# Moving the affine map of five norms from GpSimd to VectorE, one stage later, in a two-block transformer kernel

## The chip, the cores and the metric

The kernel runs on one core of a Trainium2 chip, in one launch. The metric is the device time of one execution in microseconds (us); lower is better. Times are medians of several executions. Five engines share the work: TensorE (PE in the rows; the loading of its stationary operand is PEld), VectorE (DVE), ScalarE (ACT), GpSimd (POOL) and SyncE (SP), which here only issues DMAs. Each engine executes its own instructions in order and waits on semaphores for the others.

## What is computed

512 tokens of 1024 channels go through six residual stages with a layer norm each (a first block of depth 2) and then through a second block whose details the change does not touch:

```python
for i in range(2):
    y = mla(x) if i == 0 else dsa(x)            # latent attention / sparse attention
    x = layer_norm(ALPHA * x + y, ln_g[i, 0], ln_b[i, 0])
    y = memory_cross_attention(x, mem, ...)     # 4 heads of 256 over 256 memory tokens
    x = layer_norm(ALPHA * x + y, ln_g[i, 1], ln_b[i, 1])
    y = swiglu_ffn(x, ...)
    x = layer_norm(ALPHA * x + y, ln_g[i, 2], ln_b[i, 2])
return second_block(x, ...)                     # modulation, gated attention and pooling, conv FFN, final norm
# layer_norm(x, g, b) = (x - mean) * rsqrt(var + eps) * g + b
```

All of it is float32. Every large product is made of three passes with operands split into a high and a low part (`wh`/`wl` for weights), so that the product keeps float32 precision.

## The kernel before

The residual stream `xs` is four tiles of [128 tokens, 1024]. The output projection of a stage (`out_proj`, called by `block_out` or, for the last one of the first block, by `run`) has the tokens on the partitions. It runs over all k but the last five (eight for that last one) with the four token tiles side by side in PSUM, and then finishes the tiles one by one, so that a tile's statistics, norm and transposes lie beside the products of the next tile. `ln_stats` adds the residual to the product (`x<-x,acc`, line 203) and takes mean and variance on VectorE; `ln_rest` has ScalarE normalise the tile in place. The tile is then (x - mean) * rstd, without g and b.

The gain and the shift are then applied twice, to two copies. The transposed copy `xT`, which feeds the next stage's products, gets them by feature when it is evicted (`t_group`, ScalarE). The residual tiles themselves get them by `affine`, lines 748 to 751: for each tile one multiply by `lg` (line 750) and one add of `lb` (line 751), both [128, 1024] float32 on GpSimd. `lg` and `lb` are rows broadcast over the partitions, and `ln_rows` (lines 744, 745) loads them by DMA from ScalarE's queue. Nothing reads the affine residual tiles before the next output projection adds them to its product, except the sparse attention, which stores them to DRAM (`spill`, line 1072, SP's queue), frees their pages, and reloads them with `xload` (line 737) at its end.

`affine` is called in five places for the first block's norms 0 to 4: twice in `xa` (the cross attention), twice in `ffn`, and once in `dsa`. In the program's order it stands behind the last step of `xa`, and behind `fm_first` (the first four products of a stage) in `ffn` and `dsa`. The Tile scheduler places it by its dependencies; on GpSimd nothing else stands ahead of it in `xa`.

Weights arrive in 512 KB pages on SP's queue (`raw`), ScalarE rounds them to `wh` (line 121) and VectorE subtracts to get `wl` (line 122; in some stages GpSimd does it). `use` and `ensure` keep four units prepared ahead of TensorE. `split` does the same to activations: ScalarE casts (lines 160 or 163), VectorE subtracts (lines 161 or 164). In `xa` the steps are: four head-halves of q by `fm_first`, then `s1(h)` (scores, line 155 among others, row maximum on VectorE, exponential on ScalarE), `norm(h)` (line 876, VectorE), `s2(h)` (transposes, split) and `s3(h)` (values).

Of the kernel before, what the change touches and what calls it, by code (L numbers as in the profile page):

```python
# [14 lines left out]
OP = mybir.AluOpType  # L15
# [16 lines left out]
# where steps of the memory's keys and values go between the heads (MLA) or the blocks of queries (sparse attention),  # L32
# and where the products of the second half's values (MLA) and of the pooled channels go between the heads
# [31 lines left out]
class K:  # L65
# [29 lines left out]
    def after(self, inst, prev):  # L95
        """Keep inst behind prev on their engine."""
        self.tc.add_manual_dep(inst.ins, prev.ins.name,
                               mybir.DependencyInfo(mybir.DependencyClass.NoSync, mybir.DependencyReason.SCHED_ONLY),
                               reason="order")

# [66 lines left out]
    def rsqrt_ops(self, v, n, eps, ops, out):  # L167
        """out = (v + eps) ** -0.5 on [128, n], as a list of steps."""
# [42 lines left out]
    def ln_rest(self, mv, x):  # L211
        """Steps from the statistics to the normalised tile."""
# [8 lines left out]
    def t_group(self, xs, xT, grp, gb):  # L221
        """Steps: transposes of token tiles 2*grp, 2*grp+1, then the affine map by feature, then the split."""
# [35 lines left out]
    def out_proj(self, nk, lhs, stats, rest, xT, tr, gb, last=5):  # L258
        """lhs(k): function of the token tile, the two parts; tr: the tiles that are transposed."""
# [6 lines left out]
        for k in range(nk - last):  # L266
            lp = lhs(k)
            u = self.use()
            for t in range(NT):
                mm(t, k, lp, u)  # L270
        lps = [lhs(k) for k in range(nk - last, nk)]
        us = [self.use(0) for _ in range(last)]
        self.ensure(self.cur + 4)

# [24 lines left out]
    def fm_first(self, xT, xs, gb, jobs):  # L299
        """jobs: functions(ps) that take the finished [128, 512] product."""  # L300
# [46 lines left out]
    def trig(self):  # L347
        """cos and signed sin of the rotary angles, [128 = (.., 2, 16), S]."""
# [25 lines left out]
    def rope(self, src, out):  # L374
        """Rotate [128 = (4, 2, 16), S] (in PSUM or SBUF), split into the pair out."""
# [284 lines left out]
    def attention(self, nh, rows, vals, OT, scale, ahead, before3=None, fill=None, lag=3):  # L660
        """Causal attention of heads of 64."""
# [86 lines left out]
    def affine(self, xs, rows):  # L748
        for x in xs:
            self.nc.gpsimd.tensor_tensor(x, x, rows[0], op=OP.mult)  # L750
            self.nc.gpsimd.tensor_tensor(x, x, rows[1], op=OP.add)
# [13 lines left out]
    def block_out(self, n, nk, lhs, xs):  # L765
        """Output product, residual and norm n; the normalised tiles stay in xs, their transposes begin."""
# [3 lines left out]
                      xT, xs, gb)  # L770
        return xT, gb

# [58 lines left out]
    def fill(self, n=1):  # L831
        """Some steps of the memory's keys and values, between other work."""
# [10 lines left out]
    def xa(self, i, xT, xs, gb, KT, V):  # L843
# [9 lines left out]
        rows = self.ln_rows(3 * i)  # L853
# [67 lines left out]
        self.affine(xs, rows)  # L921
        return OT

# [1 line left out]
    def ffn(self, xT, xs, gb, rows=None, step=None, conv=None):  # L925
# [32 lines left out]
        if rows is not None:  # L958
            self.affine(xs, self.ln_rows(rows))
# [95 lines left out]
    def dsa(self, xT, xs, gb):  # L1055
# [13 lines left out]
        self.affine(xs, self.ln_rows(2))  # L1069
# [25 lines left out]
        # scores of the keys, and their choice  # L1095
# [55 lines left out]
        # keys, values, queries  # L1151
# [34 lines left out]
        # attention: rows (4 groups of 4 queries, 4 queries, 2 key heads, 4 query heads of each), 16 queries at a time  # L1186
# [5 lines left out]
        def qblk(s):  # L1192
            """The queries of 64 tokens by blocks, as steps."""
# [132 lines left out]
    def bias_tables(self):  # L1326
        """Thresholds by (query % 4, bucket) and group of 4 queries; steps of the bias table in three bfloat16 parts,
        one block for each query."""
# [49 lines left out]
    def second(self, xT, xn, xs):  # L1378
# [9 lines left out]
        # pooling over trailing windows  # L1388
# [23 lines left out]
        # forget gates  # L1412
# [23 lines left out]
        # values  # L1436
# [117 lines left out]
    def run(self):  # L1554
# [12 lines left out]
        xT, gb = self.block_out(1, 8, self.cols(OT), xs)  # L1567
# [4 lines left out]
        lhs = self.ffn(xT, xs, gb, 1, self.mod_step)  # L1572
        xT, gb = self.block_out(2, NF, lhs, xs)
# [4 lines left out]
        xT, gb = self.block_out(3, 8, lhs, xs)  # L1578
# [4 lines left out]
        xT, gb = self.block_out(4, 8, self.cols(OT), xs)  # L1583
# [4 lines left out]
        lhs = self.ffn(xT, xs, gb, 4, self.mod_step)  # L1588
# [15 lines left out]
        self.out_proj(NF, lhs, lambda t, acc: self.ln_stats(t, acc, xs[t]), rest, xT, xn, self.modgb(0), 8)  # L1604
# [9 lines left out]
def layout(inputs):  # L1614
    """The arrays that the program reads: inputs, some with their rows or columns regrouped, and constants."""
# [45 lines left out]
```

## Time and profile before

| | before |
|---|---|
| runs | 2223.41, 2224.93, 2235.49 us; median 2224.93 us |
| span of the profiled execution | 2221.3 us |
| median over that span | 3.6 us |
| TensorE busy | 2153.8 us (97%) |
| VectorE busy | 1378.0 us (62%) |
| ScalarE busy | 899.0 us (40%) |
| GpSimd busy | 415.9 us (19%) |

The profile's own execution has no time beside its span; the 3.6 us are what the median of the runs has above it, start and end of the execution included. All positions below are microseconds from the span's start. The stages that the change touches lie at 320 to 375 us (first cross attention) and 375 to 415 (its output projection), 415 to 700 and 700 to 785 (first feed-forward and its output projection), 815 to 1110 and 1114 to 1160 (sparse attention), 1186 to 1240 and 1240 to 1285 (second cross attention), 1285 to 1534 and 1534 to 1650 (second feed-forward). A row of a group names the engine, the line, the operation, the tile written and the tiles read. In the timeline a bracket gives how long the engine had been idle before the instruction and what it had waited for. PEclk is the granted clock of TensorE as a share of 2.4 GHz.

### The profile page before, as it was taken

Reading aid. Unit: us, or ns where it says so; the run is one execution under the profiler, and the core shown is the slowest. Engines: PE = TensorE matmul, PEld = TensorE weight load, DVE = VectorE, ACT = ScalarE, POOL = GpSimd, SP = SyncE. Lnnn points to the kernel's source line nnn. Section 1 sums busy time; section 2 is a strip of 40 time slices with the busy share of each in tenths; the row PEclk is TensorE's granted clock in tenths of the full one; section 3 lists DMA queues with packets and bytes.
Section 4 is the critical chain, followed back from the end, with each engine's and each line's share of the span. In section 5 each row is a group of like instructions: output and inputs, shape, how many; then the busy total and the mean of one; then the engine's idle time right before and its main releaser. Section 6 shows DMA issues by size and latency. Waiting matters only on the chain.

```text
span 2221.3 us, 30434 instructions
## 1 busy us (share of the span) xinstructions
PE 2153.8 (97%) x11668; PEld 1806.4 (81%) x11668; DVE 1378.0 (62%) x2779; ACT 899.0 (40%) x1636; POOL 415.9 (19%) x330
## 2 busy tenths in 40 slices
PE   8899998999999999889998999999999999999998
PEld 7789897888888887776588898888888879888886
DVE  5776567575335269898866575435477676755633
ACT  3687344322234143456633342224323555433521
POOL 0355112040000024365504030000004210000002
PEclk9999999999999998999999999999999999999999
DMA  5223622264324214231242336544410144433311
GB/s 194 57 65 101 196 81 90 71 203 145 103 86 142 63 45 123 64 113 39 81 133 76 95 113 209 162 134 142 114 49 22 52 124 143 125 104 95 123 67 39
DMA packets 253394, 232.29 MB, mean 105 GB/s; under 512 B 14656, under 2 KB 219840, under 8 KB 253248
## 3 DMA queue, kind: packets, MB, share of 16 engines
q1 hardware_dynamic: 246240, 213.93, 31.4%
q10 hardware_dynamic: 7008, 16.41, 2.3%
q8 instruction: 92, 1.51, 0.3%
q14 instruction: 54, 0.44, 0.1%
HBM read 220.80 MB, written 6.82 MB: 102 GB/s over the span
## 4 chain that ended last, share of the span: by engine, by line
PE 82%; DVE 8%; issue 2%; ACT 1%; POOL 1%; DMA 0%; ACTq 0%; DVEq 0%; POOLq 0%
PE fm L154 13%; PE fm L153 13%; PE fm L155 13%; PE acc L154 9%; PE acc L153 9%; PE acc L155 9%; DVE wl L122 1%; PE v L153 1%; PE o L153 1%; PE v L154 1%; PE o L154 1%; PE v L155 1%; PE o L155 1%; PE s L1232 1%; PE s L155 1%
## 5 line engine op out<-in xcount | busy, mean ns | idle before, releaser
L154 PE MATMUL fm<-xT,wh 128*128 128x512 f32 (+3 forms) x1640 | 590.6, 362 | 0.4
L155 PE MATMUL fm<-xT,wl 128*128 128x512 f32 (+3 forms) x1640 | 589.9, 360 | 0.0
L153 PE MATMUL fm<-xT,wh 128*128 128x512 f32 (+3 forms) x1640 | 589.6, 361 | 0.1
L122 DVE TENSOR_TENSOR wl<-raw,wh 128x1024 fp32r<-128x1024 f32 (+1 forms) x299 | 399.7, 1365 | 113.2 <-ACT wh L121 75.0
L121 ACT CAST wh<-raw 128x1024 fp32r<-128x1024 f32 (+2 forms) x339 | 338.7, 1039 | 62.9 <-PE acc L154 19.7
L154 PEld LDWEIGHTS fm<-xT,wh 128*128 128x128 f32 (+2 forms) x1640 | 308.4, 188 | 48.4 <-DVE xT L250 1.6
L155 PEld LDWEIGHTS fm<-xT,wl 128*128 128x128 f32 (+2 forms) x1640 | 308.7, 188 | 47.3
L153 PEld LDWEIGHTS fm<-xT,wh 128*128 128x128 f32 (+2 forms) x1640 | 307.8, 188 | 48.0 <-DVE xT L249 0.4
L153 PE MATMUL acc<-wh,hs 128*128 128x512 f32 x528 | 205.6, 389 | 0.0
L155 PE MATMUL acc<-wh,hs 128*128 128x512 f32 x528 | 205.4, 389 | 0.0
L154 PE MATMUL acc<-wl,hs 128*128 128x512 f32 x528 | 205.4, 389 | 0.0
L750 POOL TENSOR_TENSOR x<-x,lg 128x1024 f32<-128x1024 f32 x20 | 60.5, 3045 | 720.8 <-DMA lg<-in_ln_g_dram 625.9
L122 POOL TENSOR_TENSOR wl<-raw,wh 128x1024 fp32r<-128x1024 f32 (+1 forms) x40 | 94.0, 2359 | 409.9 <-DVE ss L1370 327.5
L955 DVE TENSOR_TENSOR hT<-sil,fm 128x512 f32<-128x512 f32 x44 | 30.2, 686 | 194.7 <-PE fm L155 194.7
L954 ACT ACTIVATE sil<-fm 128x512 f32<-128x512 f32 x44 | 26.3, 599 | 293.9 <-PE fm L155 285.3
L938 DVE SCALAR_TENSOR_TENSOR cv<-fm,cw,cv 128x511 f32<-128x511 f32 x88 | 65.7, 748 | 81.9 <-ACT cv L936 80.7
L155 PEld LDWEIGHTS acc<-wh,hs 128*128 128x128 f32 x528 | 99.1, 188 | 20.6
L153 PEld LDWEIGHTS acc<-wh,hs 128*128 128x128 f32 x528 | 99.1, 188 | 20.6
L154 PEld LDWEIGHTS acc<-wl,hs 128*128 128x128 f32 x528 | 99.1, 188 | 20.4
L153 PE MATMUL acc<-wh,ot 128*128 128x512 f32 x288 | 112.5, 391 | 0.0
L155 PE MATMUL acc<-wh,ot 128*128 128x512 f32 x288 | 112.1, 389 | 0.0
L154 PE MATMUL acc<-wl,ot 128*128 128x512 f32 x288 | 112.0, 389 | 0.0
(366 smaller groups left out, 3738.0 us busy)
## 6 DMA issues: line engine op xcount, KB each, us to landing
raw<-in_ffn_w_in_dram SPq DMA_DIRECT2D x88, 512.0 KB, 4.0
mw<-in_mod_w_dram SPq DMA_DIRECT2D x48, 512.0 KB, 4.5
raw<-in_ffn_w_down_dram SPq DMA_DIRECT2D x44, 512.0 KB, 3.3
raw<-in_ffn_up_dram SPq DMA_DIRECT2D x44, 512.0 KB, 4.0
raw<-in_xa_w_kv_dram SPq DMA_DIRECT2D x32, 512.0 KB, 3.9
raw<-in_ffn_down_dram SPq DMA_DIRECT2D x22, 512.0 KB, 3.3
raw<-in_xa_w_q_dram SPq DMA_DIRECT2D x16, 512.0 KB, 5.8
raw<-in_xa_w_o_dram SPq DMA_DIRECT2D x16, 512.0 KB, 3.8
```

Of the source, the lines that this page charges most:

```text
L121: self.nc.scalar.copy(hi[:, :n], raw[:, :n])
L122: self.lo_eng.tensor_tensor(lo[:, :n], raw[:, :n], hi[:, :n].bitcast(F), op=OP.subtract)
L153: mm(out, l[0], r[0], start=first, stop=False, **kw)
L154: mm(out, l[0], r[1], start=False, stop=False, **kw)
L155: mm(out, l[1], r[0], start=False, stop=last, **kw)
L750: self.nc.gpsimd.tensor_tensor(x, x, rows[0], op=OP.mult)
L938: nc.vector.scalar_tensor_tensor(y[:, sh:], p[:, :S - sh], w[:, 2 - sh, c:c + 1], y[:, sh:], op0=OP.mult, op1=OP.add)
L954: nc.scalar.activation(s, g, AF.Silu)
L955: nc.vector.tensor_tensor(hT[j // 2][:, j % 2], s, u, op=OP.mult)
L1232: mm(p[32 * gq:32 * gq + 32, 0:nk], D3[:, i, hf], mv[:, gq, 0:nk], start=False, stop=i == 2, skip_group_check=True)
```

## The change

`affine` moves to VectorE. `xa`, `ffn` and `dsa` no longer call it; instead `out_proj` takes a list `pre` with one step for each tile. It executes one step after each k of its first loop and the remaining ones ahead of the products that finish the tiles. The rows `lg` and `lb` are loaded where the output projection begins. In `dsa` the tiles are now spilled without the affine map, and get it after the reload. The core of the diff (comments and docstrings, which the change also removes, left out, so lines behind them move by a few):

```diff
     def affine(self, xs, rows):
         for x in xs:
-            self.nc.gpsimd.tensor_tensor(x, x, rows[0], op=OP.mult)
-            self.nc.gpsimd.tensor_tensor(x, x, rows[1], op=OP.add)
+            self.nc.vector.tensor_tensor(x, x, rows[0], op=OP.mult)
+            self.nc.vector.tensor_tensor(x, x, rows[1], op=OP.add)
+
+    def affine_of(self, xs, n):
+        if n is None:
+            return None
+        rows = self.ln_rows(n)
+        return lambda t: self.affine(xs[t:t + 1], rows)
...
-    def out_proj(self, nk, lhs, stats, rest, xT, tr, gb, last=5):
+    def out_proj(self, nk, lhs, stats, rest, xT, tr, gb, last=5, pre=None):
+        pre = [] if pre is None else [lambda t=t, f=pre: f(t) for t in range(NT)]
...
             for t in range(NT):
                 mm(t, k, lp, u)
+            if pre:
+                pre.pop(0)()
         lps = [lhs(k) for k in range(nk - last, nk)]
         us = [self.use(0) for _ in range(last)]
         self.ensure(self.cur + 4)
+        for f in pre:
+            f()
...
-    def block_out(self, n, nk, lhs, xs):
+    def block_out(self, n, nk, lhs, xs, prev=None):
...
-                      xT, xs, gb)
+                      xT, xs, gb, pre=self.affine_of(xs, prev))
...
         self.fm_first(xT, xs, gb, [take(m) for m in range(4)])      # xa
-        rows = self.ln_rows(3 * i)
...
         s3(3)
-        self.affine(xs, rows)
...
-        if rows is not None:                                        # ffn
-            self.affine(xs, self.ln_rows(rows))
...
         self.fm_first(xT, xs, gb, [take_qi(m) for m in range(4)])   # dsa
-        self.affine(xs, self.ln_rows(2))
         spill = self.tc.dram_tile([NT, 128, D], F, name="spill")
...
-        xT, gb = self.block_out(1, 8, self.cols(OT), xs)
+        xT, gb = self.block_out(1, 8, self.cols(OT), xs, 0)
...
-        lhs = self.ffn(xT, xs, gb, 4, self.mod_step)
+        lhs = self.ffn(xT, xs, gb, self.mod_step)
+        pre = self.affine_of(xs, 4)
         rows = self.ln_rows(5)
```

What this does to the order of the instructions: TensorE's order stays as it was but for one exchange of neighbours. GpSimd loses the 40 instructions of lines 750 and 751; VectorE gains 40 of the same shape (lines 756 and 757 in the changed file).

The first place is VectorE in the output projection of the first cross attention. `ot` are the last splits of the attention, `wl` the low parts of weights: the first four (from raw_3628 to raw_3964) are units 4 to 7 of this projection, the other four belong to the next stage. Before:

```order
543 L161 TENSOR_TENSOR ot_3931<-o_3924,ot_3931 128x512
544 L161 TENSOR_TENSOR ot_3941<-o_3934,ot_3941 128x512
545 L122 TENSOR_TENSOR wl_3961<-raw_3628,wh_3960 128x1024
546 L122 TENSOR_TENSOR wl_3991<-raw_3714,wh_3990 128x1024
547 L122 TENSOR_TENSOR wl_4021<-raw_3766,wh_4020 128x1024
548 L122 TENSOR_TENSOR wl_4051<-raw_3964,wh_4050 128x1024
549 L122 TENSOR_TENSOR wl_4057<-raw_3994,wh_4056 128x1024
550 L122 TENSOR_TENSOR wl_4063<-raw_4024,wh_4062 128x1024
551 L122 TENSOR_TENSOR wl_4069<-raw_4054,wh_4068 128x1024
552 L122 TENSOR_TENSOR wl_4075<-raw_4060,wh_4074 128x1024
553 L203 SCALAR_TENSOR_TENSOR x_2836<-x_2836,acc_3952 128x512
```

And now, where the same four units are wl_3953, wl_3985, wl_4017 and wl_4049:

```order
544 L161 TENSOR_TENSOR ot_3937<-o_3930,ot_3937 128x512
545 L756 TENSOR_TENSOR x_2836<-x_2836,lg_3940 128x1024
546 L122 TENSOR_TENSOR wl_3953<-raw_3624,wh_3952 128x1024
547 L757 TENSOR_TENSOR x_2836<-x_2836,lb_3941 128x1024
548 L122 TENSOR_TENSOR wl_3985<-raw_3710,wh_3984 128x1024
549 L756 TENSOR_TENSOR x_2838<-x_2838,lg_3940 128x1024
550 L122 TENSOR_TENSOR wl_4017<-raw_3762,wh_4016 128x1024
551 L757 TENSOR_TENSOR x_2838<-x_2838,lb_3941 128x1024
552 L756 TENSOR_TENSOR x_2840<-x_2840,lg_3940 128x1024
553 L122 TENSOR_TENSOR wl_4049<-raw_3956,wh_4048 128x1024
554 L757 TENSOR_TENSOR x_2840<-x_2840,lb_3941 128x1024
555 L122 TENSOR_TENSOR wl_4055<-raw_3988,wh_4054 128x1024
```

The first affine instruction stands ahead of every `wl` of this stage, and the eight affine instructions are spread between the eight `wl`.

The second place is VectorE where the second feed-forward goes over to its output projection. `hT` is the feed-forward's product of gate and value (its last half, line 955 before and 967 now), `hs` its split, which is the stationary operand of the projection. Before:

```order
1895 L122 TENSOR_TENSOR wl_14187<-raw_14070,wh_14186 128x1024
1896 L1049 SCALAR_TENSOR_TENSOR modcol<-modcol,col_99 128x8
1897 L161 TENSOR_TENSOR hs_14232<-hT_12474,hs_14232 128x512
1898 L161 TENSOR_TENSOR hs_14235<-hT_12474,hs_14235 128x512
1899 L161 TENSOR_TENSOR hs_14238<-hT_12475,hs_14238 128x512
1900 L122 TENSOR_TENSOR wl_14242<-raw_14101,wh_14241 128x1024
1901 L161 TENSOR_TENSOR hs_14271<-hT_12475,hs_14271 128x512
1902 L955 TENSOR_TENSOR hT_12484<-sil_14217,fm_14192 128x512
```

And now:

```order
1930 L1059 SCALAR_TENSOR_TENSOR modcol<-modcol,col_99 128x8
1931 L756 TENSOR_TENSOR x_10958<-x_10958,lg_14208 128x1024
1932 L756 TENSOR_TENSOR x_10960<-x_10960,lg_14208 128x1024
1933 L757 TENSOR_TENSOR x_10958<-x_10958,lb_14209 128x1024
1934 L757 TENSOR_TENSOR x_10960<-x_10960,lb_14209 128x1024
1935 L967 TENSOR_TENSOR hT_12484<-sil_14205,fm_14180 128x512
1936 L161 TENSOR_TENSOR hs_14224<-hT_12474,hs_14224 128x512
1937 L161 TENSOR_TENSOR hs_14227<-hT_12474,hs_14227 128x512
1938 L161 TENSOR_TENSOR hs_14230<-hT_12475,hs_14230 128x512
1939 L122 TENSOR_TENSOR wl_14234<-raw_14089,wh_14233 128x1024
1940 L161 TENSOR_TENSOR hs_14265<-hT_12475,hs_14265 128x512
```

Four affine instructions have come in, and the last `hT`, which waits for the last product of the feed-forward, now stands ahead of the first `hs` instead of behind the fourth.

The third place is SP's queue at the start of the sparse attention, where `spill` stores the residual tiles and `raw` are its weights. Before:

```order
161 L113 DMA raw_6935<-in_dsa_w_dram 128x4x256
162 L113 DMA raw_6941<-in_dsa_w_dram 128x4x256
163 L113 DMA raw_7230<-in_dsa_w_dram 128x8x128
164 L113 DMA raw_7236<-in_dsa_w_dram 128x8x128
165 L1072 DMA spill<-x_2836 128x1024
```

And now:

```order
161 L1081 DMA spill<-x_2836 128x1024
162 L1081 DMA spill<-x_2838 128x1024
163 L1081 DMA spill<-x_2840 128x1024
164 L113 DMA raw_6935<-in_dsa_w_dram 128x4x256
165 L113 DMA raw_6941<-in_dsa_w_dram 128x4x256
166 L1081 DMA spill<-x_2842 128x1024
167 L113 DMA raw_7218<-in_dsa_w_dram 128x8x128
```

The stores, which waited for GpSimd, stand four queue places earlier and wait only for ScalarE's normalisation.

## Rows read from the trace of the kernel before

**Rows 1.** the page's part 1: busy us (share of the span) xinstructions.

```profile
PE 2153.8 (97%) x11668; PEld 1806.4 (81%) x11668; DVE 1378.0 (62%) x2779; ACT 899.0 (40%) x1636; POOL 415.9 (19%) x330
```

**Rows 2.** the page's part 4: the chain that ended last, by engine.

```profile
PE 82%; DVE 8%; issue 2%; ACT 1%; POOL 1%; DMA 0%; ACTq 0%; DVEq 0%; POOLq 0%
```

**Rows 3.** groups of GpSimd: line, form xcount | busy us, mean ns | idle us.

```profile
L122 POOL TENSOR_TENSOR wl<-raw,wh 128x1024 fp32r<-128x1024 f32 x39 | 93.7, 2411 | 82.4 <-ACT wh L121 55.1 <-issue 13.6 <-DVE mk L1217 11.7
L751 POOL TENSOR_TENSOR x<-x,lb 128x1024 f32<-128x1024 f32 x20 | 61.4, 3092 | 0.1
L750 POOL TENSOR_TENSOR x<-x,lg 128x1024 f32<-128x1024 f32 x20 | 60.5, 3045 | 720.8 <-DMA lg<-in_ln_g_dram 625.9 <-ACT P L870 94.9
```

**Rows 4.** groups of VectorE, 322 to 355 us (first cross attention).

```profile
L122 DVE TENSOR_TENSOR wl<-raw,wh 128x1024 fp32r<-128x1024 f32 x5 | 14.1, 2837 | 0.0
```

**Rows 5.** groups of VectorE, 375 to 415 us (its output projection).

```profile
L122 DVE TENSOR_TENSOR wl<-raw,wh 128x1024 fp32r<-128x1024 f32 x8 | 9.2, 1220 | 0.3 <-ACT wh L121 0.3
```

**Rows 6.** timeline, 335 to 346 us: start us, us, instruction [idle before <-releaser].

```profile
335.22 6.69 DVE L122 TENSOR_TENSOR wl<-raw,wh 128x1024 fp32r<-128x1024 f32 x2
...
337.14 0.60 ACT L163 ACTIVATE q<-fm 128x512 fp32r<-128x512 f32 x1 [3.97 <-PE fm L155]
...
337.87 0.28 PE L154 MATMUL s<-k,q 128*128 128x256 f32 x1
...
341.84 0.68 DVE L164 SCALAR_TENSOR_TENSOR q<-fm,q 128x512 fp32r<-128x512 f32 x1
...
342.57 0.58 PE L155 MATMUL s<-k,q 128*128 128x256 f32 x1 [4.42 <-DVE q L164]
...
345.87 0.58 PE L155 MATMUL s<-k,q 128*128 128x256 f32 x1 [2.29 <-DVE q L164]
```

**Rows 7.** waits of TensorE, two cross attentions: total us, times, longest us.

```profile
PE s L155 <- DVE q L164: 6.7, 2, 4.4
...
PE s L155 <- DVE q L164: 6.6, 2, 4.3
```

**Rows 8.** windows: stretch, us, busy of PE, PEld, DVE, ACT, POOL; PEclk, DMA share, GB/s.

```profile
341.80:352.00 10.20, 7.14 (x27) 6.46 (x28) 7.57 (x9) 2.90 (x9) 7.97 (x3) 0.50 0.00 0
1205.40:1215.60 10.20, 5.76 (x24) 5.37 (x25) 7.57 (x8) 1.96 (x5) 9.34 (x4) 0.50 0.00 0
829.90:833.30 3.40, 3.40 (x9) 2.26 (x8) 2.76 (x3) 2.10 (x4) 3.40 (x2) 0.50 0.33 134
847.00:864.00 17.00, 16.36 (x38) 9.14 (x38) 16.62 (x35) 8.02 (x16) 2.91 (x5) 0.50 0.24 56
```

**Rows 9.** timeline of the sparse attention's start, VectorE and TensorE.

```profile
818.87 7.91 DVE L122 TENSOR_TENSOR wl<-raw,wh 128x1024 fp32r<-128x1024 f32 x3 [0.24 <-ACT wh L121]
...
828.74 0.41 PE L1091 MATMUL pw<-cst,wsb 8*128 8x8 f32 x4 [1.79 <-ACT wsb L1087]
```

**Rows 10.** timeline of VectorE, end of the first cross attention's output projection.

```profile
401.34 1.37 DVE L203 SCALAR_TENSOR_TENSOR x<-x,acc 128x512 f32<-128x512 f32 x2 [11.70 <-PE acc L155]
...
408.14 1.37 DVE L203 SCALAR_TENSOR_TENSOR x<-x,acc 128x512 f32<-128x512 f32 x2 [1.67 <-PE acc L155]
```

**Rows 11.** the DMAs of lines 744 and 745 (rows lg and lb), to landing.

```profile
DMA to landing us min/median/max: 3.6/3.6/4.6
...
DMA to landing us min/median/max: 5.6/6.5/7.4
```

**Rows 12.** timeline of VectorE, output projection of the sparse attention.

```profile
1118.41 6.90 DVE L122 TENSOR_TENSOR wl<-raw,wh 128x1024 fp32r<-128x1024 f32 x6 [2.27 <-ACT wh L121]
1127.27 1.23 DVE L122 TENSOR_TENSOR wl<-raw,wh 128x1024 fp32r<-128x1024 f32 x1 [1.96 <-ACT wh L121]
...
1137.27 1.37 DVE L203 SCALAR_TENSOR_TENSOR x<-x,acc 128x512 f32<-128x512 f32 x2 [6.97 <-PE acc L155]
```

**Rows 13.** timeline at the start of the second feed-forward's output projection.

```profile
1534.18 0.39 PE L153 MATMUL acc<-wh,hs 128*128 128x512 f32 x1
...
1534.38 0.69 DVE L955 TENSOR_TENSOR hT<-sil,fm 128x512 f32<-128x512 f32 x1 [0.49 <-PE fm L155]
```

More of the change, by code (lines that the diff above doesn't have):

```diff
@@ L920, in xa, with ffn @@
         s3(3)
-        self.affine(xs, rows)
         return OT
-    def ffn(self, xT, xs, gb, rows=None, step=None, conv=None):
+    def ffn(self, xT, xs, gb, step=None, conv=None):
         nc = self.nc
@@ L1571, in run @@
         self.mod_start()
-        lhs = self.ffn(xT, xs, gb, 1, self.mod_step)
-        xT, gb = self.block_out(2, NF, lhs, xs)
+        lhs = self.ffn(xT, xs, gb, self.mod_step)
+        xT, gb = self.block_out(2, NF, lhs, xs, 1)
         if self.stop == "x02":
@@ L1577, in run @@
         lhs, xs = self.dsa(xT, xs, gb)
-        xT, gb = self.block_out(3, 8, lhs, xs)
+        xT, gb = self.block_out(3, 8, lhs, xs, 2)
         if self.stop == "x10":
@@ L1582, in run @@
         OT = self.xa(1, xT, xs, gb, *self.kv1)
-        xT, gb = self.block_out(4, 8, self.cols(OT), xs)
+        xT, gb = self.block_out(4, 8, self.cols(OT), xs, 3)
         if self.stop == "x11":
@@ L1587, in run @@
         self.mlimit = 40
-        lhs = self.ffn(xT, xs, gb, 4, self.mod_step)
+        lhs = self.ffn(xT, xs, gb, self.mod_step)
+        pre = self.affine_of(xs, 4)
         rows = self.ln_rows(5)
@@ L1603, in rest @@
             return ops + self.rms_rest(xs[t], xn[t], ss[t])
-        self.out_proj(NF, lhs, lambda t, acc: self.ln_stats(t, acc, xs[t]), rest, xT, xn, self.modgb(0), 8)
+        self.out_proj(NF, lhs, lambda t, acc: self.ln_stats(t, acc, xs[t]), rest, xT, xn, self.modgb(0), 8,
+                      pre)
         if self.stop == "x12":
```

## The prediction

> **What bounds the kernel now.** I read the page first: TensorE is busy for 2153.8 us of 2221.3, 97% [rows 1], and the chain that ended last runs over it for 82% [rows 2]. So time can only be won where TensorE waits or runs at its lower clock, and lost where something new makes it wait. The next view was the groups of GpSimd: the 40 affine instructions take 60.5 + 61.4 = 121.9 us there, 3.05 and 3.09 us each [rows 3]. Nothing in the chain needs them, so their own time is worth nothing. What is worth something is what they do to VectorE. While they run in the first cross attention, a `wl` subtraction takes 2.84 us on VectorE [rows 4]; the same shape takes 1.22 us in the stage behind, where GpSimd is idle [rows 5]. Then I went to the timeline at that place and to the list of TensorE's waits. Two such `wl` take 6.69 us from 335.22 and a third follows; the `q` split, whose ScalarE half was done at 337.74, therefore starts at 341.84, and TensorE, which came to the scores at 337.87, stands for 4.42 and then for 2.29 us [rows 6]. The second cross attention has the same pair [rows 7]. Right behind both waits the granted clock is 0.50, the 1.2 GHz level, for 10.2 us [rows 8]. The sparse attention begins in the same way, with three `wl` in 7.91 us and a wait of 1.79 us [rows 9], then two stretches at 0.50 [rows 8].
>
> **Part 1: GpSimd no longer works beside the cross attentions.** Put the `wl` at 1.22 us: the two that end at 341.91 would have ended before the cast of `q` (337.74), so VectorE takes `q` at once, 0.68 us, and ends near 338.4; TensorE wants it at 338.15. That leaves about 0.4 us of the 4.42. The next `q` comes behind one more `wl` (338.4 + 1.22 + 0.68 = 340.3), while TensorE, having done three short matmuls, arrives near 339.2: about 1.1 us is left of the 2.29. So 1.5 of 6.65 us stays, and 5.15 us go in each stage, 10.3 in both. The low clock: in the two stretches TensorE is busy for 7.14 and 5.76 us at half speed [rows 8], so the same work at 2.4 GHz takes 3.57 and 2.88 us less, 6.45 together, provided the clock no longer falls. Bounds for this part: the waits alone and the clock as before, -10.3; no residue at all, -13.3 - 6.45 = -19.7. I take **-16.75**. What is late next is the 1.5 us of `q`, behind VectorE's own queue.
>
> **Part 2: the sparse attention's start.** The three `wl` shrink to 3.66 us, 4.25 less than now, which is more than the 1.79 us that TensorE waits [rows 9], so that wait goes; and with it the stretch of 3.4 us at 0.50, where TensorE is busy throughout: half, 1.7 us [rows 8]. Sum **-3.5**. The longer stretch, 847 to 864, has no large wait ahead of it; TensorE is busy for 16.36 of its 17 us with small products [rows 8]. I leave it as it is; if it went too, it would give 16.36 / 2 = 8.2 us more. The spill, which left SP's queue behind the affine map, now goes ahead of two weight loads; the pages it frees come sooner, and the 512 KB loads behind it are shifted by its issue only. I count it as nothing.
>
> The Trainium skill (SBUF — State Buffer, "Who interferes with whom") says that GpSimd and VectorE contend for one shared port pair by an exclusive lock, the loser waiting out the other's whole instruction. For two `wl` this gives 2 x (2.4 + 1.22) = 7.2 us where the row has 6.69 [rows 6], so the trace about agrees. By that rule two `wl` that GpSimd itself does here (2.41 us each [rows 3]), which come earlier now, would stop VectorE for 4.8 us in the indexer; if TensorE felt all of it the sum below would be 4.8 us higher. In the sum it stands at nothing, since no wait of TensorE for VectorE stands there now.
>
> **Part 3: the five output projections.** Each gets 8 instructions of [128, 1024] on VectorE. GpSimd is idle there, so the row for one is 1.22 us [rows 5]: 9.8 us a stage, 49 in all. The bound above is the 2.84 us of a disturbed one [rows 4]; below 1.22 nothing speaks for a gain. The cover, in the first cross attention's projection: VectorE is idle for 11.70 us before 401.34 [rows 10]. The first affine instruction stands ahead of all `wl` and waits for `lg`, which lands 3.6 to 4.6 us after its issue [rows 11]. Its last `wl` ends at 401.34 - 11.70 = 389.64. So VectorE ends at most at 389.64 + 4.6 + 9.8 = 404.0, 2.7 us past 401.34; the next tile comes 6.80 us after the first, with 1.67 us idle ahead of it [rows 10], so the lag dies out over two tiles, and TensorE first needs a normalised tile behind the third one. The `wl` queued behind the waiting instruction: unit 7, the last that this stage needs, is the ninth instruction from the start. The eight `wl` begin at 389.64 - 9.5 = 380.1 now [rows 5], so this row begins near 384 and unit 7 ends near 384 + 9 x 1.22 = 395; TensorE wants it for the end of the block that ends at 401.34 and lasts 6.8 us, so near 400. Slack 5 us: **0**. The second cross attention is the same. In the first feed-forward's projection, which lasts twice as long, also 0.
>
> In the sparse attention's projection the affine map waits besides for the reloaded tiles, issued on ScalarE's queue ahead of `lg`; VectorE's idle is 2.27 + 1.96 + 6.97 = 11.2 us [rows 12]. If `lg` is issued when the first `wl` starts now, 1118.41, it lands near 1122; 9 `wl` and 8 affine instructions from there take 20.7 us, to 1142.7: 5.4 us past 1137.27. At 1.67 us recovered for each tile the lag is gone at the fourth, and the transposes wait for the first two tiles only. I take **+0.5**, bounds 0 and 5.4.
>
> The second feed-forward's projection is the one place where the order itself costs. TensorE's first `acc` matmul starts at 1534.18, straight behind the last product; the last `hT` starts at 1534.38 [rows 13] and then stood behind the first `hs`. Now `hs` stands behind `hT`: 1534.38 + 0.69 + 0.69 = 1535.8 for the first one, so TensorE waits about 1.5 us. The bounds are 0 (had the scheduler's order no effect) and 1.5 + 1.7, if the clock falls as it did behind the wait of 1.79 us in part 2. I take **+1.5**.
>
> **Sum.** -16.75 - 3.5 + 0.5 + 1.5 = -18.25 on a span of 2221.3, that is 2203.05. The median of the runs lies 3.6 us above the profiled span, so 2206.7 us; I say 2206.5.
>
> **Rivals.**
> - *The clock stays low in the cross attentions.* The residual 1.5 us and the short matmuls of the scores are still there, and so may be the stretches at 0.50. For it: in the sparse attention the clock fell behind a wait of 1.79 us, and from 847 to 864 with hardly any [rows 8, 9]. Against: 4.42 us is far more than 0.4. It gives back 6.45 + 1.7: 2206.7 + 8.2 = 2214.9. The Trainium skill (TensorE: Matmul & The Clock Gate, Part 1) has the low clock as the default that activity lifts; the rows show only 0.50 and full there, which agrees with it.
> - *The sparse attention's long stretch recovers too*, since VectorE feeds the indexer sooner: 2206.7 - 8.2 = 2198.5. Against it: TensorE is not waiting there.
> - *GpSimd was not the cause*: another load on SBUF stretches the `wl`, or `q` is held by something else. Then parts 1 and 2 give nothing, part 3 costs its 2 us: 2227. Against it the two durations in [rows 4, 5].
> - *VectorE becomes the bound of the output projections* (slower). Mechanism: the eight affine instructions and the `wl` between them run at the disturbed 2.84 us instead of 1.22, now against the weight DMAs. Unit 7 is then done at 384 + 9 x 2.84 = 409.6 where TensorE wants it at 400: 9.6 us of waiting and some 3.2 us of low clock, as in part 1, in each of five stages: 64 us, 2271. TensorE starts to wait when one takes (400 - 384) / 9 = 1.8 us; slower than before by 11 us overall it is when five stages cost 18 + 11 = 29 us, that is 2.6 us of wait and 3.2 of clock each, at 2.07 us. Against it: the eight `wl` at 1.22 us in the same place with weights streaming [rows 5]. The Trainium skill (Perfetto Trace Analysis, "Optimizing Scalar/DVE Operations") says that with a saturated VectorE work may go to GpSimd; 62% busy [rows 1] is not saturated.
>
> **How the numbers follow.** A change of less than 0.5%, 11 us, can't be told from none. Forecast (2206.5, its own range 2200 to 2212): 0.54. Clock stays low: 0.15, at 2214.9 just within 0.5%, so a third of it counts as faster. Long stretch recovers: 0.14. GpSimd not the cause: 0.11. VectorE the bound: 0.06. Faster: 0.54 + 0.14 + 0.05 = 0.73; same: 0.10 + 0.11 = 0.21; slower: 0.06. The range takes in the clock on both sides, with some us for terms 1 and 3: 2196 to 2217; it leaves out the last two rivals, 0.17.
>
> **What would show it.** Right: `wl` on VectorE at 1.22 us in the cross attentions, their waits for `q` below 2 us together, full clock from 337 to 352 and its counterpart; no wait of `pw`; GpSimd idle there. TensorE waiting about 1.5 us for `hs` at the start of the second feed-forward's projection, and for no `wl` in any. Wrong: a wait of TensorE for `wl` or `x` in an output projection, VectorE's affine instructions above 1.8 us, or stretches at 0.50 that come back elsewhere with the time unchanged.

## The result, and the profile after

The changed kernel takes 2199.33 us (median of 4 runs, 2198.14 to 2203.36) against 2230.21 us for the kernel before in the same comparison (4 runs in all, 2223.41 to 2236.6). The ratio is 0.987, 95% interval 0.9845 to 0.9902: faster by 1.0 to 1.6%. Runs of the kernel before lie at two levels, near 2224 and near 2235 us, and two of these four were at the upper one; against its median of 2224.61 in the 25 runs beside the first experiments the changed kernel is 1.1% faster. The profiled spans are 2196.2 and 2221.3 us, a difference of 25.1 us, also 1.1%.

First the page of the changed kernel, part 1 and the chain, which answer to [rows 1, 2]:

```profile
PE 2144.8 (98%) x11668; PEld 1798.5 (82%) x11668; DVE 1353.9 (62%) x2819; ACT 898.8 (41%) x1636; POOL 294.2 (13%) x290
...
PE 85%; DVE 6%; issue 1%; ACT 1%; POOL 1%; DMA 0%; ACTq 0%; SPq 0%; DVEq 0%; POOLq 0%
```

VectorE has 40 instructions more and is busy for 24.1 us less: 49 us of new work came in, and its old work shrank by more than that. TensorE's 11668 instructions are the same and stand in the same order but for nine (the exchange is of these nine, not of two neighbours), so the two traces can be laid over each other instruction by instruction. The difference in start grows in five places: by 10.1 us in the first cross attention (the first matmuls behind the scores start at 352.1 before and at 341.3 after, with 0.8 us of lead from earlier), by 3.8 us at the start of the sparse attention (3.3 of them up to 840 us of the kernel before), by 9.3 us in the second cross attention, and by 1.5 us in the second block and 0.8 us before 90 us, two places that the change does not touch and where stretches of low clock lie elsewhere or are missing. In the first feed-forward 0.3 us are lost again.

The windows of the changed kernel show the two cross attentions and the start of the sparse attention (columns as in [rows 8]):

```profile
311.00:364.00 53.00, 52.99 (x327) 47.28 (x327) 31.41 (x45) 24.49 (x59) 0.00 (x0) 1.00 0.27 86
1175.00:1225.00 50.00, 49.99 (x265) 42.60 (x264) 29.35 (x40) 27.73 (x59) 0.00 (x0) 1.00 0.35 113
816.30:820.00 3.70, 3.70 (x18) 2.50 (x18) 1.72 (x4) 2.30 (x5) 0.71 (x1) 1.00 0.00 0
832.20:849.20 17.00, 17.00 (x37) 9.06 (x37) 13.22 (x31) 5.78 (x11) 0.00 (x0) 0.50 0.02 4
```

GpSimd does nothing in the cross attentions, TensorE is busy throughout at full clock, and the last row is the long stretch at 0.50 of the sparse attention, as long as before, only earlier. The timeline there, which answers to [rows 6]:

```profile
331.52 0.69 DVE L164 SCALAR_TENSOR_TENSOR q<-fm,q 128x512 fp32r<-128x512 f32 x1
332.45 1.23 DVE L122 TENSOR_TENSOR wl<-raw,wh 128x1024 fp32r<-128x1024 f32 x1 [0.24 <-ACT wh L121]
337.02 0.69 DVE L164 SCALAR_TENSOR_TENSOR q<-fm,q 128x512 fp32r<-128x512 f32 x1 [3.34 <-ACT q L163]
...
337.77 0.39 PE L155 MATMUL s<-k,q 128*128 128x256 f32 x1
```

Before, VectorE was behind everyone in this stretch; now it is idle for 3.34 us ahead of the second `q` split and waits for ScalarE. The added work, in the first cross attention's and then in the sparse attention's output projection (these answer to [rows 10, 12]):

```profile
374.75 1.22 DVE L756 TENSOR_TENSOR x<-x,lg 128x1024 f32<-128x1024 f32 x1 [5.42 <-DMA lg<-in_ln_g_dram]
...
391.79 1.22 DVE L757 TENSOR_TENSOR x<-x,lb 128x1024 f32<-128x1024 f32 x1
392.92 1.28 DVE L203 SCALAR_TENSOR_TENSOR x<-x,acc 128x512 f32<-128x512 f32 x2
...
1110.15 1.23 DVE L756 TENSOR_TENSOR x<-x,lg 128x1024 f32<-128x1024 f32 x1 [8.68 <-DMA lg<-in_ln_g_dram]
...
1128.33 1.28 DVE L203 SCALAR_TENSOR_TENSOR x<-x,acc 128x512 f32<-128x512 f32 x2
```

All 20 multiplies take 1.215 to 1.226 us. In both places VectorE does wait for `lg`, 5.42 and 8.68 us, and the statistics then follow the affine map without a gap, so they are late: TensorE is 10.9 and 14.7 us earlier there than before, and against [rows 10, 12] so shifted the first statistics come 2.5 and 5.7 us later (the prediction had 2.7 at most and 5.4). TensorE waits in none of the five output projections for `wl`, `x` or `hs`.

### The profile page after: what moved, and what is told of

Same layout as the page of the kernel before. It is cut to its first block, busy times and chain, and to the rows that moved or that the text cites. A ratio compares the mean times of both kernels' runs of the same rounds, so it can differ in the third digit from the quotient of the medians.

```text
span 2196.2 us, 30394 instructions
## 1 busy us (share of the span) xinstructions
PE 2144.8 (98%) x11668; PEld 1798.5 (82%) x11668; DVE 1353.9 (62%) x2819; ACT 898.8 (41%) x1636; POOL 294.2 (13%) x290
## 4 chain that ended last, share of the span: by engine, by line
PE 85%; DVE 6%; issue 1%; ACT 1%; POOL 1%; DMA 0%; ACTq 0%; SPq 0%; DVEq 0%; POOLq 0%
PE fm L154 14%; PE fm L153 14%; PE fm L155 14%; PE acc L154 9%; PE acc L155 9%; PE acc L153 9%; PE v L153 1%; PE v L154 1%; PE o L153 1%; PE v L155 1%; PE o L154 1%; PE o L155 1%; PE s L1241 1%; PE tp L232 1%; PE s L155 1%
## 5 line engine op out<-in xcount | busy, mean ns | idle before, releaser
L122 DVE TENSOR_TENSOR wl<-raw,wh 128x1024 fp32r<-128x1024 f32 (+1 forms) x299 | 357.0, 1218 | 93.4 <-ACT wh L121 63.9
L155 PEld LDWEIGHTS acc<-wh,hs 128*128 128x128 f32 x528 | 99.1, 188 | 20.5
L217 ACT ACTIVATE x<-x,mv 128x1024 f32<-128x1024 f32 x20 | 24.9, 1243 | 147.4 <-DVE mv L216 147.4
```

What stands on the lines that cost most here:

```text
L122: self.lo_eng.tensor_tensor(lo[:, :n], raw[:, :n], hi[:, :n].bitcast(F), op=OP.subtract)
L155: mm(out, l[1], r[0], start=False, stop=last, **kw)
L217: ops.append(lambda: nc.scalar.activation(x, x, AF.Identity, bias=mv[:, 3:4], scale=mv[:, 2:3]))
```

## The experiments

Spans are those of the profiled execution; "behind" and "ahead" of another kernel are read by laying TensorE's instructions over each other. A kernel for which no ratio is given ran once, so its total weighs less than what stands at a named place of its trace. The sparse attention's rounds are its loop over blocks of queries, about 905 to 990 us.

**Only the cross attentions.** Norms 0 and 3 moved; the other three maps as before.

```diff
+        if rows is not None:
+            self.affine(xs, self.ln_rows(rows))
...
-        xT, gb = self.block_out(2, NF, lhs, xs, 1)
+        xT, gb = self.block_out(2, NF, lhs, xs)
```

(`ffn` and `dsa` call `affine` on GpSimd again)

> The changed kernel with the map moved for the norms 0 and 3 only (the two cross attentions); feed-forward and sparse attention keep theirs on GpSimd at the old place. Theory (GpSimd working beside VectorE stretches VectorE's subtractions, the split of q comes late, TensorE waits and its clock falls): the two cross attentions give 10.1 and 9.6 us as in the changed kernel, the sparse attention nothing; span about 2221.3 - 19.7 = 2201.6 us, ratio 0.991. Rival (the gain is spread over all five places, part of it in the feed-forwards): about two fifths of 25 us, 2211 us.

Measured: span 2204.0 us, ratio 0.992 (0.9906 to 0.9936). The two stages give 10.1 and 9.3 us, as in the changed kernel. Between 925 and 990 (times of the kernel before) it loses 3.9 us: the three stretches at 0.50 in the sparse attention's rounds are 27.3 us long together, before 17.0. So the theory holds in its places (19.4 of the 19.7 us expected), and the span missed 2201.6 us by low clock in a stage where this kernel differs from before only in its timing.

**Only the sparse attention.** Norm 2 moved, the others as before (the same edit the other way round).

> The changed kernel with the map moved for norm 2 only (sparse attention). Theory: the wait of pw (1.8 us), the low clock behind it (1.7 us) go, 3.5 us in all: span about 2217.8 us, ratio 0.998; both cross attentions keep their waits for q (13.3 us). Rival (a common cause outside these stages): more than 8 us less.

Measured: span 2217.8 us, ratio 0.997 (0.9959 to 0.9986). The two queries of who waited for whom, first of the kernel with the cross attentions alone, then with the sparse attention alone:

```profile
PE pw L1104 <- ACT wsb L1100: 1.8, 1, 1.8
```

```profile
PE s L155 <- DVE q L164: 13.5, 4, 4.7
```

Each keeps the wait whose map stayed, and lacks the other (`pw` are four small transposes of TensorE at the start of the sparse attention). The spans give 17.3 + 3.5 = 20.8 of the 25.1 us; most of the rest is the 3.9 us of low clock in the first of the two kernels.

**The engine without the place.** The kernel before with `affine` on VectorE, called where it was.

```diff
-            self.nc.gpsimd.tensor_tensor(x, x, rows[0], op=OP.mult)
-            self.nc.gpsimd.tensor_tensor(x, x, rows[1], op=OP.add)
+            self.nc.vector.tensor_tensor(x, x, rows[0], op=OP.mult)
+            self.nc.vector.tensor_tensor(x, x, rows[1], op=OP.add)
```

> The kernel before with the two instructions of the map on VectorE at the old places; nothing else moved. Theory (the engine is what matters): wl on VectorE at 1.22 us in the cross attentions, and 9.8 us more of VectorE there; the q splits stand behind one or two more instructions, so TensorE waits 0 to 2.5 us a stage instead of 6.65: 15 to 20 us less than before, span 2201 to 2206 us. Rival (the place matters: whatever executes the map inside the cross attention delays q): waits for q of 5 us or more a stage, span above 2214 us.

Measured: ratio 0.997 (0.9953 to 0.9993), span 2222.6 us: both theories fail on the total: the waits are the theory's, the span is the rival's. The profiled run took 2224.52 us, the median of its ten runs is 2220.62. TensorE's waits, then windows of the first cross attention and of the sparse attention's start:

```profile
PE pw L1091 <- ACT wsb L1087: 7.5, 1, 7.5
...
PE s L155 <- DVE q L164: 2.6, 2, 1.8
```

```profile
821.70:872.90 51.20, 45.77 (x101) 26.64 (x102) 29.97 (x60) 15.86 (x30) 8.36 (x7) 0.50 0.29 76
322.00:376.00 54.00, 52.16 (x288) 44.98 (x287) 42.33 (x54) 28.12 (x63) 0.00 (x0) 1.00 0.42 127
```

In the cross attentions the theory holds: waits of 1.8 us in one stage and 0.8 in the other, full clock, 8.3 and 8.5 us won. In the sparse attention the eight instructions stand in VectorE's queue ahead of the `wl` and `kid`, from 812.48 to 821.76 (`kid` are the keys by which the sparse attention chooses); `pw` waits 7.5 us, and 51 us at 0.50 follow: 15.7 us lost up to the end of that stretch, and 4.1 more in the rounds. So there the place is what matters.

**The place without the engine.** The changed kernel with `affine` on GpSimd.

```diff
-            self.nc.vector.tensor_tensor(x, x, rows[0], op=OP.mult)
+            self.nc.gpsimd.tensor_tensor(x, x, rows[0], op=OP.mult)
```

(and the add likewise)

> The changed kernel with the map at its new place, in the output projections, but on GpSimd again. Theory (load on GpSimd stretches VectorE, and costs only where TensorE is near to VectorE): wl in the projections goes from 1.22 to 2.4 to 3.4 us, the first statistics come some us late, but TensorE has the cover worked out in the prediction, so the span is within 3 us of the changed kernel, 2196 to 2199 us. Rival (any GpSimd load beside VectorE costs TensorE time, wherever it stands): waits of TensorE for wl or hs in the projections, 10 us or more above the changed kernel.

Measured: ratio 0.9975 (0.9964 to 0.9987), span 2216.0 us, 19.8 us behind the changed kernel: 11.1 in the first feed-forward's projection, 6.9 in the sparse attention's, 1.8 in the second feed-forward's and none in the cross attentions' two. The theory's cover was wrong in three of five places; there the rival holds. The waits, then VectorE and GpSimd where the first feed-forward goes over to its projection:

```profile
PE acc L153 <- DVE hT L967: 8.1, 1, 8.1
...
PE tp L232 <- ACT x L217: 4.1, 1, 4.1
```

```profile
655.42 7.08 DVE L161 TENSOR_TENSOR hs<-hT,hs 128x512 fp32r<-128x512 f32 x3 [1.37 <-ACT hs L160]
662.43 3.40 DVE L122 TENSOR_TENSOR wl<-raw,wh 128x1024 fp32r<-128x1024 f32 x1
665.76 2.83 DVE L161 TENSOR_TENSOR hs<-hT,hs 128x512 fp32r<-128x512 f32 x1
668.51 3.35 DVE L122 TENSOR_TENSOR wl<-raw,wh 128x1024 fp32r<-128x1024 f32 x1
671.79 0.68 DVE L967 TENSOR_TENSOR hT<-sil,fm 128x512 f32<-128x512 f32 x1
```

```profile
659.11 5.64 POOL L756 TENSOR_TENSOR x<-x,lg 128x1024 f32<-128x1024 f32 x2
664.71 6.08 POOL L757 TENSOR_TENSOR x<-x,lb 128x1024 f32<-128x1024 f32 x2
```

```profile
672.52 0.80 PE L153 MATMUL acc<-wh,hs 128*128 128x512 f32 x1 [8.07 <-DVE hT L967]
```

An `hs` of 0.68 us takes 7.08 / 3 = 2.36, a `wl` of 1.22 takes 3.40: the price beside GpSimd, 1.7 and 2.2 us, goes by the instruction more than by its size, so many short ones are hit hardest. `hT`, queued behind them, reads the feed-forward's last product out of PSUM. TensorE had done seven of the projection's first eight products when the eighth had to wait for it; that the eighth takes over the PSUM buffer that `hT` reads (the program has eight) is inferred from the program, the trace shows the wait alone.

**GpSimd's load put back, without the data.** The changed kernel, with unused multiplies on GpSimd in each cross attention.

```diff
+        rows = self.ln_rows(3 * i)
+        for _ in range(8):
+            nc.gpsimd.tensor_tensor(rows[0], rows[0], rows[1], op=OP.mult)
```

> The changed kernel with 8 multiplies of [128, 1024] put back on GpSimd in each cross attention at the old place; they multiply the two rows lg and lb with each other and nothing reads their result. Theory: the waits of TensorE for q come back (about 6.6 us a stage), and the low clock behind them, so 19.7 us more than the changed kernel: span about 2216 us. Rival (the residual tiles' dependencies or the order around the map held q, not the load on GpSimd): within 1 us of the changed kernel, 2196 us, though GpSimd is as busy there as before.

Measured: span 2218.9 us, ratio to before 0.998 (0.9964 to 0.9992). Waits and GpSimd's timeline:

```profile
PE s L155 <- DVE q L164: 10.8, 4, 3.8
```

```profile
328.62 24.01 POOL L869 TENSOR_TENSOR lg<-lg,lb 128x1024 f32<-128x1024 f32 x8 [98.68 <-DMA lb<-in_ln_b_dram]
```

```profile
342.20:349.00 6.80, 6.19 (x24) 5.80 (x25) 4.17 (x6) 2.96 (x9) 6.64 (x3) 0.50 0.00 0
1205.80:1212.60 6.80, 5.09 (x22) 4.90 (x23) 4.17 (x7) 1.96 (x5) 6.59 (x3) 0.50 0.00 0
```

Load alone brings back 10.8 of the 13.3 us of waiting, and a stretch at 0.50 of 6.8 us behind the waits in each stage (10.2 before), together 16.3 of the 19.4 us that the two stages had given; it began 3.5 us later than the map did, since it waits for `lb` too. The rest of the 22.7 us behind the changed kernel is low clock elsewhere. The dependencies of the residual tiles are not needed for the effect.

**The same in the sparse attention**, `rows = self.ln_rows(2)` and the same eight multiplies.

> The changed kernel with 8 multiplies of the two rows with each other on GpSimd at the old place in the sparse attention; nothing reads them, and the spill doesn't wait for them. Theory (GpSimd's load delayed kid and pw): the wait of pw comes back, 1 to 2 us, and the low clock behind it, so 2 to 4 us above the changed kernel, 2198 to 2200 us. Rival (the gain of 3.5 us came from the spill leaving SP's queue sooner): no wait of pw, 2196 us.

Measured: span 2206.6 us, no wait of `pw`; the multiplies began at 812.39 with the landing of `lb`, when the three `wl` were nearly done (3.50 us for three). It slowed the scores behind them instead (4.7 us of waiting for `rl`, ScalarE's evictions of the scores). It doesn't tell the theories apart, so it was repeated with the `lg` row multiplied by itself, which starts earlier:

> As the earlier kernel with unused multiplies in the sparse attention, but each multiplies the lg row by itself, so that they start when lg has landed and not 3.6 us later with lb. Theory (GpSimd's load delayed the three wl, kid and pw): wl at 2 us or more, a wait of pw of 1 to 2 us, and TensorE's waits for rl behind it; 5 us or more above the changed kernel. Rival (the spill's place on SP's queue gave the gain): wl delayed, but no wait of pw.

Measured: span 2205.1 us. VectorE, and the window behind the wait:

```profile
808.47 6.90 DVE L122 TENSOR_TENSOR wl<-raw,wh 128x1024 fp32r<-128x1024 f32 x3 [0.25 <-ACT wh L121]
```

```profile
819.80:823.20 3.40, 3.40 (x8) 2.28 (x8) 1.90 (x3) 1.08 (x3) 3.24 (x3) 0.50 0.00 0
```

The three `wl` take 6.90 us (7.91 in [rows 9], 3.5 without load), `pw` waits 0.8 us, and 3.4 us at 0.50 follow it as they did before [rows 8]. The wait is less than the 1 to 2 expected, its direction and what follows it are the theory's. Up to 840 us of the kernel before, 2.3 of the 3.3 us that the changed kernel gains there are lost again although the spill leaves early in this kernel, so the spill's place can have given 1.0 us at most. The rest of the 8.9 us above the changed kernel is longer low clock behind it, in the long stretch (20.5 us) and in the rounds (30.7 us).

**GpSimd that only writes.** Unused memsets in each cross attention:

```diff
+        ghost = self.pg(F, "lg")
+        for _ in range(24):
+            nc.gpsimd.memset(ghost, 0.0)
```

> The changed kernel with 24 memsets of a [128, 1024] page on GpSimd in each cross attention, at the old place; nothing reads the page. They write SBUF and read nothing. Theory A (any GpSimd access to SBUF holds VectorE): wl at 2 us or more while they last, waits of TensorE for q of 2 us or more a stage. Theory B (only GpSimd's reads meet VectorE's second read): wl at 1.22 us, no wait for q, span within 1 us of the changed kernel.

Measured: span 2206.4 us. With no DMA to wait for they began at 295.20, too early for the `wl`; what lay beside them were the splits of `xT`. Groups of VectorE from 290 to 318 us, first with memsets, then in the changed kernel:

```profile
L249 DVE CAST xT<-ysc 128x256 fp32r<-128x256 f32 x16 | 9.4, 610 | 4.5 <-ACT ysc L241 4.5
L250 DVE TENSOR_TENSOR xT<-ysc,xT 128x256 fp32r<-128x256 f32 x16 | 6.3, 417 | 0.1
```

```profile
L250 DVE TENSOR_TENSOR xT<-ysc,xT 128x256 fp32r<-128x256 f32 x16 | 6.3, 420 | 0.1
L249 DVE CAST xT<-ysc 128x256 fp32r<-128x256 f32 x16 | 4.4, 288 | 5.6 <-ACT ysc L241 5.4
```

The cast with one input doubles, the subtraction with two stays. TensorE waited 1.8 and 1.5 us for `xT` in the two stages, which lost 3.9 and 4.8 us there; the `q` and `wl` behind were undisturbed. So as to have the memsets beside the `wl`, they were put behind one multiply that waits for `lg`:

> The changed kernel with one multiply and then 21 memsets (1.03 us each) on GpSimd in each cross attention, from the landing of lg on, so that they lie beside the wl and q splits. Theory A (any GpSimd access to SBUF holds VectorE's subtractions): wl 2 us or more and TensorE waits for q. Theory B (only GpSimd's reads hold VectorE's instructions with two SBUF inputs; the first memsets stretched the one-input cast of xT, 0.61 for 0.29 us, but not the subtraction beside it): wl 1.22 us but for one or two beside the multiply, no wait for q, within 2 us of the changed kernel outside the sparse attention's rounds.

Measured: span 2198.7 us, 2.5 above the changed kernel, and no wait for `q`. GpSimd and VectorE:

```profile
328.14 21.24 POOL L870 MEMSET lg<- 128x1024 f32 x21
```

```profile
331.56 2.35 DVE L122 TENSOR_TENSOR wl<-raw,wh 128x1024 fp32r<-128x1024 f32 x2
```

Theory B: beside the memsets a `wl` takes its 1.18 us. So GpSimd's being busy, or its writing, did not hold VectorE in the kernel before. A memset and a multiply differ in more than what they read; that it is the reading is the nearest explanation, not one that these two kernels separate from others.

**Nothing in place of the map.** The changed kernel without the 40 instructions; gain and shift on the residual path are left out.

```diff
-        return lambda t: self.affine(xs[t:t + 1], rows)
+        return lambda t: None
```

> The changed kernel without the 40 instructions of the map on the residual tiles (the rows are still loaded): leaves out gain and shift on the residual path for norms 0 to 4, so what it computes is not the reference. Theory (the 49 us of VectorE in the projections are covered): within 1 us of the changed kernel, 2195 to 2197 us. Rival (they cost TensorE something in the projections): 3 us or more below it.

Measured: span 2198.7 us, ratio to before 0.9885 (0.9862 to 0.9908). It isn't below the changed kernel's 2196.2: its low clock lies elsewhere, before 90 us and in the sparse attention's rounds. Over each of the five output projections TensorE takes as long in both kernels (0.4 us longer without the map in the last, equal in the others). The 49 us on VectorE cost nothing that shows, and nothing more is to be had from the map.

**TensorE's passes in the old order.** The three passes of a product kept together at the start of the second feed-forward's projection, by an order dependency from each product's last pass to the next one's first:

```diff
+                if last == 8 and k == 0:
+                    if st:
+                        self.after(a, st[0])
+                    st[:] = [z]
```

> The changed kernel with TensorE's order at the start of the second feed-forward's projection as it was before: the three passes of a product behind one another, instead of the first two passes of four products ahead of their third passes. Theory (this exchange of nine instructions is what hid the late hs that the prediction priced at 1.5 us): TensorE waits about 1.1 us for hs there, and the rest of that stage is 1 us later. Rival (hs isn't late at all): no wait.

Measured: span 2200.1 us; TensorE waits at that place, and is 1.3 us further behind the changed kernel after it:

```profile
1514.25 0.50 PE L155 MATMUL acc<-wh,hs 128*128 128x512 f32 x1 [1.00 <-DVE hs L161]
```

By chance this run also shows how thin the cover of the sparse attention's projection is. VectorE, and TensorE's wait there:

```profile
1113.59 1.22 DVE L761 TENSOR_TENSOR x<-x,lg 128x1024 f32<-128x1024 f32 x1 [10.70 <-DMA lg<-in_ln_g_dram]
```

```profile
PE acc L154 <- DVE wl L122: 0.4, 1, 0.4
```

With 10.70 us of waiting for `lg` instead of 8.68, TensorE waits 0.4 us for a `wl` queued behind it. (In the kernel with the 24 memsets the wait for `lg` was 10.6 us, and TensorE waited 0.3.)

**The changed kernel once more.**

> The changed kernel once more, to see how far the stretches of low clock move between two profiles of the same program. Theory: the waits are the same to 0.5 us; the stretches at 0.50 in the sparse attention's rounds (907 to 965) and in the second block differ by up to 4 us in all.

Measured: span 2196.6 us. In the sparse attention's rounds the stretches at 0.50 did not move: they are the same three, 10.2, 3.4 and 3.4 us long, at 907.8, 935.1 and 962.4 instead of 907.3, 934.6 and 961.9. So they came out alike in two profiles of one program, while the other experiments have 20 to 31 us there, against 17.0 in this one and in the kernel before. Two profiles don't show that they always repeat.

## Why the prediction was right, and where its terms were off

It forecast 2206.5 us from a span of 2203.05; the span came out at 2196.2 and the time at 2199.33. That is inside 2196 to 2217, but just below the forecast's own 2200 to 2212: the wide bounds hold it because they took in the rival of the long stretch that recovers (2198.5), and that did not happen. So the mechanism and the places were right, and that the time lies beside that rival's is chance. The 6.9 us between the spans are 2.7 in part 1, 0.3 in part 2, 2.0 in part 3 and 1.9 of low clock in other places. By its own steps:

- **Part 1, -16.75: right in mechanism, measured -19.4** (10.1 and 9.3), near the end of its bounds. The term that failed is the residue of 1.5 us a stage. I put the `q` split at 341.84 [rows 6] with the cast that ends at 337.74. It belongs to the cast before, at 331.64, as the shapes of the queue show (two casts, then two splits); on the late VectorE the pair had drifted 10 us apart, and the split of the cast at 337.14 was the next one, at 345.14. Without the load the first split is done at 332.2 and only the second has to follow its cast at once. TensorE doesn't wait for either. The `q` split itself, which has one input in PSUM, took 0.68 us beside GpSimd [rows 6] and 0.69 without; what was stretched were instructions with both inputs in SBUF, and only beside GpSimd's multiplies and adds (2.36 us for an `hs` of 0.68), not beside its memsets (1.18 us for a `wl`). The Trainium skill (SBUF — State Buffer, "Who interferes with whom") says that a VectorE instruction with two SBUF inputs "contends with a GpSimd instruction that reads SBUF", and not with one that only writes it; these durations agree. For one with a single SBUF input the same section has contention in a 2-port mode; the cast of 0.61 for 0.29 us beside memsets would fit that, but whether it ran in such a mode no run shows.
- **Part 2, -3.5: measured -3.3, and 0.5 more in the long stretch.** The wait of `pw` and the 3.4 us at 0.50 behind it went, the long stretch stayed 17 us long, as the prediction had it; the 0.5 is a wait of 0.6 us for `rl` that also went. The unused load brought a part of the wait, and the same stretch, back. The 4.8 us that the prediction feared from GpSimd's own two `wl` did not come: beside the second, at 820.06, three `sc` instructions of VectorE took 3.51 us (0.48 each alone), and TensorE waited for none of them.
- **Part 3, +0 and +0.5: measured 0.** The waits for `lg` were longer than the 3.6 to 4.6 us of [rows 11] allow for (landing took 3.4 to 8.0 us, and VectorE was idle for 5.42 and 8.68), and the cover still held: without the map the kernel is no faster. It was closer than I had it, since 2 us more of that wait already reach TensorE. In the sparse attention `lg` was issued right behind the four reloads of the residual tiles; that these made it land later is likely, but no run shows it.
- **Part 3, +1.5 in the second feed-forward: measured 0.** `hs` is as late as predicted, three of them take from 1511.08 to 1512.97 and TensorE's first `acc` starts at 1510.20. But the exchange in TensorE's order, which I had passed over, stands at this very place:

```profile
1510.20 0.39 PE L153 MATMUL acc<-wh,hs 128*128 128x512 f32 x1
1510.43 0.39 PE L154 MATMUL acc<-wl,hs 128*128 128x512 f32 x1
1510.65 0.39 PE L153 MATMUL acc<-wh,hs 128*128 128x512 f32 x1
...
1512.01 1.07 PE L155 MATMUL acc<-wh,hs 128*128 128x512 f32 x4
```

  The third pass alone reads the low part of `hs`, which VectorE makes last. TensorE's new order puts eight matmuls of the first two passes ahead of it, 1.81 us of work. With the passes in the old order the wait is there, 1.0 us. It is less than 1.5 because the prediction held the first `hs` against TensorE's first matmul, and the one that needs it, the third pass, comes two matmuls later, 0.45 us.
- **The rivals.** The clock did not stay low in the cross attentions, the long stretch did not recover, and GpSimd was the cause. That VectorE becomes the bound did not happen: beside the weight DMAs the multiplies took 1.22 us. With GpSimd's load there its mechanism is real: `wl` at 3.4 us, 8.1 us of waiting at one place.

Of the 25.1 us, 23.2 are in the three stages named. The rest, 1.9 us, is low clock before 90 us and in the second block, less the 0.3 us lost in the first feed-forward. In the second block it is one stretch of 3.4 us, at 1795.9 before, that the changed kernel and its repeat don't have; of the other kernels three have it at the same place of the program (the sparse attention alone, and the first two with unused multiplies), the rest don't. Why it is there in one program and not in another, and why the stretches in the sparse attention's rounds differ, stays open.

## What to carry to other kernels

Work on an idle engine isn't free when it shares something with one that the bound waits for: compare the duration of the same instruction beside it and without it, and count how many instructions of the other engine lie beside it. An engine and a place are chosen together: each half of this change was worth 0.3%, the whole 1.1 to 1.3%. And when orders are compared, an exchange of a few instructions is to be read at the place where a wait is predicted: here it was what removed the wait.

## What the runs showed of the hardware that was not expected

- A VectorE instruction with two SBUF inputs beside GpSimd's two-input ones takes up to some 1.7 to 2.2 us longer, whatever its own length (0.68 to 2.36, 1.22 to 3.40). GpSimd's own take 2.8 to 3.1 us in the mean there instead of the 2.4 that is their shortest.
- A GpSimd memset of [128, 1024] takes about 1 us (24.64 us for 24), leaves such instructions alone, and doubles a one-input cast of VectorE.
- A wait of 0.8 us was followed by 3.4 us at the 1.2 GHz level in the sparse attention, while waits of 1.8 and 0.8 us in the cross attentions (the map on VectorE at the old place) were not. And the changed kernel's long stretch at 0.50 has no wait ahead of it at all: from 800 to 862 TensorE waits for nothing, and in these 17.00 us it counts as busy for all 17.00, with 37 products. Why is open.
